# One instruction order for every engine at the start of a two-block model, and the last attention's mask as an identity matmul

## The chip, the core and the metric

The kernel runs on one core of a Trainium2 chip. The core has five engines with a queue of instructions each: TensorE (matmuls and their weight loads, PE and PEld in the profile), VectorE (DVE), ScalarE (ACT), GpSimd (POOL) and SyncE (SP, which issues DMAs). Each works through its queue in order and waits on semaphores for the others. The metric is the time of one execution in microseconds (us); lower is better.

## The reference

Two transformer blocks on 512 tokens with 1024 channels in float32. What matters here is the first line of the first block, a normalization of x, and the last mixer, a "stick-breaking" attention with 16 heads of 64 channels:

```python
def rms_norm(x, g):
    xf = x.astype(jnp.float32)
    xf = xf * lax.rsqrt(jnp.mean(xf * xf, axis=-1, keepdims=True) + EPS)
    return (xf * g.astype(jnp.float32)).astype(x.dtype)
# first block: h = rms_norm(x, norm1_g); z = h @ w_in; GLU and causal convolution, a dilated
# window attention (softmax), gates, then a feed-forward part. Second block: an attention on
# the 128 best keys, then this one:
def stick_breaking_mixer(x, w_in, w_out):
    q, k, v, g = jnp.split(x @ w_in, 4, axis=-1)        # each to 16 heads of 64
    z = jnp.einsum('bqhd,bshd->bhqs', qb, k) * HEAD_DIM_2 ** -0.5
    before = pos[None, :] < pb[:, None]                  # strictly earlier keys
    log_one_minus = jnp.where(before, jax.nn.log_sigmoid(-z), 0.0)
    log_stick = lax.cumsum(log_one_minus, axis=3, reverse=True) - log_one_minus
    a = jnp.where(before, jnp.exp(jax.nn.log_sigmoid(z) + log_stick), 0.0)
    o = jnp.einsum('bhqs,bshd->bqhd', a, v)
    return (o * jax.nn.silu(g)) @ w_out
```

## The kernel before

Activations stand as 8 tiles of 128 channels by 512 tokens. For accuracy each float32 operand is held as two float32r tiles, a rounded high part (`Ah`, `whi`) and the rest (`Al`, `wlo`), and a product of 128 by 512 takes 8 chunks of three matmuls each (high by high, high by low, low by high; L316 to L318). Weights come in 233 blocks, most of 512 KB, in the order of use: `Weights.load_one` issues the DMA on SyncE (L86), `split_one` rounds the block on ScalarE (`whi`, L118) and subtracts on GpSimd (`wlo`, L122). Two raw blocks and four split ones have room, so a block's load waits until the block two earlier is split.

TensorE's order is written out by hand: a `Stream` holds chunks of products, and `pull(n)` emits n of them. The other engines are ordered by the framework's scheduler, except in the GLU stage, where VectorE, ScalarE and GpSimd are fixed by hand as well.

**The start.** Constants are made (L218 to L236: `ident`, the `ones` matrices, the mask `before`, which holds -1e30 at and above a diagonal). SyncE loads two weight blocks, small vectors (L454 to L465), g1 and x (four tiles of 128 tokens). For each tile ScalarE sums the squares (L439) and forms 1/sqrt by Ln and Exp (L191), VectorE scales the tile (L442), TensorE transposes it (L444). Then ScalarE and VectorE evict the eight transposed tiles times g1 as `Ah` and `Al` (L447, L448). The first product of the GLU follows, then `columns()`, which transposes the small vectors (L474 to L487), and then 15 more products with the convolution's taps beside them on VectorE and GpSimd. VectorE also builds a window table `lnc` for the first attention (L783 to L794); the first gate's Tanh takes the memory of its temporaries.

**The last loop.** Eight pairs of heads run in `pair_loop`, one head a slot. A slot takes, in this order and with chunks pulled between the steps: the scores of query tile 0, a turn of the head before, scores 1, a turn, scores 2, a turn, a weighing, scores 3, two more weighings. A score step is two matmuls into PSUM (L568, L569, high and low part of the keys, 128 to 512 columns). Then VectorE adds the mask to the 128 columns on the diagonal (L643), ScalarE takes two Sigmoids, VectorE a scan (L648) and a multiplication (L649). A turn transposes these weights on TensorE (L580) and splits them (`PTh` on ScalarE, `PTl` on VectorE, L582 and L583); a weighing multiplies them with the values (L501). Scores have two PSUM banks, which come free with the second Sigmoid.

How many chunks are pulled after each of a slot's ten steps is a table, `PULLS`: 12 a slot (`P12`) for most slots, then 12, 12, 8 and 6 in the last four. What can be pulled are the projections q, k and v of the pair two ahead, and gate products, which are placed in that stream by `GATES3`. Gates 0 to 2 are computed ahead of the loop, in halves with the normalization, gates 3 to 5 as whole products behind them, and gates 6 and 7 in the stream of the last pair.

Of the kernel before, what the change touches and what calls it, by code (L numbers as in the profile page):

```python
# [10 lines left out]
F32 = mybir.dt.float32  # L11
# [28 lines left out]
GATES3 = ((0, 0), (6, 6), (6, 6), (6, 6), (6, 6), (6, 6), (6, 6), (6, 8))  # L40
# [3 lines left out]
PULLS = ((P12, P8, P8, P6, P6), (P12, P12, P12, P12, P12), (P12, P12, P12, P8, P6))  # L44
# [103 lines left out]
def model_kernel(ctx: ExitStack, tc: tile.TileContext, x, norm1_g, w_in, gate_b, conv_w, conv_b, conv_norm_g,  # L148
# [37 lines left out]
    ordered = {"load": None, "since": []}  # L186
    no_sync = mybir.DependencyInfo(mybir.DependencyClass.NoSync, mybir.DependencyReason.DATA)

    def act(o, i, func, **kw):

        ins = nc.scalar.activation(o, i, func, **kw).ins  # L191
        if ordered["load"] is not None:
            tc.add_manual_dep(ins, ordered["load"].name, no_sync)
        ordered["since"].append(ins)

    def act_tables(name):
        ordered["load"], since = None, ordered["since"]
        ordered["since"] = []
# [21 lines left out]
    before = const.tile([128, 128], F32, name="before")  # L220
    with tc.tile_pool(name="first", bufs=1) as first:
        jp = first.tile([128, 128], I32, name="jp")
        nc.gpsimd.iota(jp, pattern=[[1, 128]], base=0, channel_multiplier=-1)
        nc.gpsimd.tensor_scalar(ident, jp, 0.0, None, op0=OP.is_equal)
        nc.vector.memset(eps6, EPS)
        nc.vector.memset(eps5, LN_EPS / (ALPHA * ALPHA))
        zero128 = first.tile([128, 128], F32, name="zero128")
        nc.vector.memset(zero128, 0.0)
        nc.vector.tensor_scalar(ones_d, zero128, 1.0 / D, None, op0=OP.add)
        nc.vector.tensor_scalar(ones_h, zero128, 2.0 / D, None, op0=OP.add)  # L230
        nc.vector.tensor_scalar(ones_b, zero128, 0.0, None, op0=OP.add)
        for r in range(2):
            a = slice(64 * r, 64 * r + 64)
            nc.vector.tensor_scalar(ones_b[a, a], zero128[a, a], 1.0 / 64, None, op0=OP.add)
        nc.gpsimd.iota(jp, pattern=[[1, 128]], base=-127, channel_multiplier=1)
        nc.vector.tensor_scalar(before, jp, 0.0, NEG, op0=OP.is_le, op1=OP.mult)  # L236

# [39 lines left out]
    add_gates(w_in_b, range(GATES3[1][0]))  # L277
# [140 lines left out]
    g1 = const.tile([128, ND], F32, name="g1")  # L418
    hT = []
# [33 lines left out]
    for j in range(2):  # L453
        nc.sync.dma_start(cr[j], conv_w[0][:, 512 * j:512 * j + 512])  # L454
# [1119 lines left out]
```

## Time and profile before

| | us |
|---|---|
| median of 3 runs | 1619.07 (1616.58 to 1619.87) |
| the profiled execution, its own time | 1622.69 |
| its span, from the first to the last instruction | 1620.9 |
| TensorE busy in the span | 1525.0 (94%) |
| VectorE | 1132.4 (70%) |
| ScalarE | 846.7 (52%) |
| GpSimd | 811.8 (50%) |
| granted TensorE clock, mean | 0.978 of full speed |

A busy time is the union of an engine's instructions. Matmuls overlap in the record: in a dense stream one starts before the bar of the one ahead of it ends, so a busy TensorE is not one at its peak, and the starts tell its pace. A wait is the idle time in front of an instruction, put down to what released it last.

### The profile page before, as it was taken

What the parts mean: (1) busy time and instruction counts of PE and PEld (TensorE: products, weight loads), DVE (VectorE), ACT (ScalarE), POOL (GpSimd) and SP (SyncE); (2) the same over time, 40 slices, a digit from 0 to 9 for tenths busy, and PEclk for the clock granted to TensorE, in tenths of its full rate; (3) what the DMA queues carried; (4) which work ended last, traced back from release to release, by engine and by line L of the source; (5) the groups of instructions that cost most, each with busy time, mean ns of one, the idle gap of its engine ahead of it and who ended that gap; (6) DMA issues with size and microseconds to landing.
All of it is one profiled execution on the core that took longest, in us unless ns stands there. A gap on an engine that the chain in (4) does not pass through costs nothing.

```text
span 1620.9 us, 21268 instructions
## 1 busy us (share of the span) xinstructions
PE 1525.0 (94%) x7806; PEld 1289.3 (80%) x7806; DVE 1132.4 (70%) x1896; ACT 846.7 (52%) x1528; POOL 811.8 (50%) x680
## 2 busy tenths in 40 slices
PE   3999889999999999999999999999999789999996
PEld 3888778887778888888888887888887678887875
DVE  5899777786246567726735669988887753888874
ACT  4445677787553344423423444366765435666652
POOL 2679963333644554454444474445542875325314
PEclk8999999999999999999999999999999799999998
DMA  3323221212133423333333242322220313212212
GB/s 110 105 78 99 84 79 54 65 54 62 44 115 101 132 81 90 91 117 92 91 107 98 80 126 65 86 71 70 61 66 14 98 58 92 66 53 66 65 39 93
DMA packets 234604, 130.36 MB, mean 80 GB/s; under 512 B 5206, under 2 KB 232774, under 8 KB 234500
## 3 DMA queue, kind: packets, MB, share of 16 engines
q1 hardware_dynamic: 234356, 128.75, 27.2%
q8 instruction: 61, 1.00, 0.2%
q14 instruction: 43, 0.35, 0.1%
q10 hardware_dynamic: 144, 0.26, 0.0%
HBM read 126.90 MB, written 2.10 MB: 80 GB/s over the span
## 4 chain that ended last, share of the span: by engine, by line
PE 46%; DVE 28%; ACT 10%; issue 7%; POOL 6%; DMA 3%; DVEq 0%; ACTq 0%; POOLq 0%
PE pj L316 8%; PE pj L318 7%; PE pj L317 7%; PE s L317 5%; PE s L316 5%; PE s L318 5%; DVE pt L819 5%; POOL wlo L122 3%; DVE rest L648 2%; DVE PTl L583 2%; PE o L501 2%; ACT whi L118 2%; POOL S L825 2%; ACT k L547 2%; DVE q L522 2%
## 5 line engine op out<-in xcount | busy, mean ns | idle before, releaser
L122 POOL TENSOR_TENSOR wlo<-wraw,whi 128x256 fp32r<-128x256 f32 (+2 forms) x548 | 659.0, 1228 | 700.4 <-ACT whi L118 655.1
L316 PE MATMUL pj<-Ah,whi 128*128 128x512 f32 (+2 forms) x880 | 356.4, 405 | 19.7 <-DVE v L706 10.0
L118 ACT CAST whi<-wraw 128x1024 fp32r<-128x1024 f32 (+3 forms) x255 | 243.9, 966 | 217.2 <-PE pj L317 73.4
L318 PE MATMUL pj<-Ah,wlo 128*128 128x512 f32 (+2 forms) x880 | 345.1, 392 | 1.8 <-POOL wlo L122 1.8
L317 PE MATMUL pj<-Al,whi 128*128 128x512 f32 (+2 forms) x880 | 344.9, 392 | 0.0
L316 PEld LDWEIGHTS pj<-Ah,whi 128*128 128x128 f32 x880 | 169.2, 192 | 46.1 <-issue 9.2
L318 PEld LDWEIGHTS pj<-Ah,wlo 128*128 128x128 f32 x880 | 167.6, 190 | 38.6 <-POOL wlo L122 3.4
L317 PEld LDWEIGHTS pj<-Al,whi 128*128 128x128 f32 x880 | 168.5, 191 | 24.2
L317 PE MATMUL s<-Al,whi 128*128 128x512 f32 (+1 forms) x368 | 141.5, 384 | 3.7 <-DVE Al L1287 3.7
L316 PE MATMUL s<-Ah,whi 128*128 128x512 f32 (+1 forms) x368 | 141.3, 384 | 3.9 <-ACT Ah L1286 3.9
L318 PE MATMUL s<-Ah,wlo 128*128 128x512 f32 (+1 forms) x368 | 140.9, 383 | 0.0
L819 DVE SCALAR_TENSOR_TENSOR pt<-S,cw,pt 128x496 f32<-128x496 f32 (+19 forms) x180 | 124.8, 736 | 5.4 <-ACT pt L812 2.8
L340 PE MATMUL pj<-whi,Ah 128*128 128x256 f32 x384 | 112.8, 294 | 1.1 <-DVE q L522 1.1
L342 PE MATMUL pj<-whi,Al 128*128 128x256 f32 x384 | 108.5, 282 | 0.0
L341 PE MATMUL pj<-wlo,Ah 128*128 128x256 f32 x384 | 108.3, 282 | 0.0
L583 DVE TENSOR_TENSOR PTl<-pt,PTh 128x512 fp32r<-128x512 f32 x144 | 85.9, 598 | 29.9 <-ACT PTh L582 29.1
L191 ACT ACTIVATE P<-P,nm 128x128 f32<-128x128 f32 (+3 forms) x128 | 72.0, 563 | 63.4 <-DVE nm L613 62.6
L732 DVE SCALAR_TENSOR_TENSOR u<-ur,fw,u 128x511 f32<-128x511 f32 x44 | 74.9, 1705 | 37.6 <-ACT u L731 37.6
L825 POOL TENSOR_TENSOR S<-S,o 128x511 f32<-128x511 f32 (+29 forms) x60 | 78.2, 1317 | 15.7 <-ACT o L824 14.6
L580 PE MATMUL pt<-ident,P 128*128 128x128 f32 x480 | 78.8, 276 | 7.7 <-DVE P L649 5.7
L317 PEld LDWEIGHTS s<-Al,whi 128*128 128x128 f32 x368 | 70.5, 192 | 17.6 <-DVE Al L1287 4.5
L316 PEld LDWEIGHTS s<-Ah,whi 128*128 128x128 f32 x368 | 70.3, 191 | 17.5 <-ACT Ah L1286 4.5
(330 smaller groups left out, 3237.1 us busy)
## 6 DMA issues: line engine op xcount, KB each, us to landing
wraw<-in_w_in_dram SPq DMA_DIRECT2D x56, 512.0 KB
wraw<-in_w_up_dram SPq DMA_DIRECT2D x44, 512.0 KB
wraw<-in_w_in_a_dram SPq DMA_DIRECT2D x36, 512.0 KB
wraw<-in_w_in_b_dram SPq DMA_DIRECT2D x32, 512.0 KB
wraw<-in_w_down_dram SPq DMA_DIRECT2D x16, 512.0 KB
wraw<-in_w_attn_out_dram SPq DMA_DIRECT2D x8, 512.0 KB
wraw<-in_w_conv_out_dram SPq DMA_DIRECT2D x8, 512.0 KB
wraw<-in_w_out_dram SPq DMA_DIRECT2D x8, 512.0 KB
```

The costliest lines, as they stand in the source:

```text
L118: nc.scalar.copy(h, s)
L122: nc.gpsimd.tensor_sub(l[:, k], s[:, k], h[:, k].bitcast(F32))
L316: nc.tensor.matmul(o, hv[:, k, :], ah, start=first, stop=False)
L317: nc.tensor.matmul(o, hv[:, k, :], al, start=False, stop=False)
L318: nc.tensor.matmul(o, lv[:, k, :], ah, start=False, stop=last)
L340: nc.tensor.matmul(o, ah, hv, start=k == 0, stop=False)
L341: nc.tensor.matmul(o, ah, lv, start=False, stop=False)
L342: nc.tensor.matmul(o, al, hv, start=False, stop=k == 7)
L580: nc.tensor.transpose(pt[:, at:at + 128], self.P[r][:, k0:k0 + 128], ident)
L583: nc.vector.tensor_sub(l[:, :at], pt[:, :at], f32(h)[:, :at])
L819: nc.vector.scalar_tensor_tensor(o, a, w, o, op0=OP.mult, op1=OP.add)
L825: nc.gpsimd.tensor_add(o, o, t)
```

## The change

It has three parts.

1. At the start all five engines get their order by hand. SyncE issues g1 and x first, then two weight blocks, then the small vectors (a function `vectors()`). The making of constants moves behind these lines in the code, and a float32r copy of `ident`, `ident_r`, is added. Of the four squares ScalarE keeps tiles 0 and 2, and VectorE takes 1 and 3. The first block's rounding is written ahead of the evictions (`W.split_one()`). A table load for ScalarE moves behind the evictions.
2. In the last attention the mask is float32r, and a matmul of `ident_r` by `before` adds it in PSUM between the two score matmuls; the addition on VectorE is gone.
3. Gates 3, 4 and 5 move from ahead of the loop into its stream, and 11 slots pull 14 chunks in place of 12 (one more behind the third turn, one more behind the last weighing).

```diff
-GATES3 = ((0, 0), (6, 6), (6, 6), (6, 6), (6, 6), (6, 6), (6, 6), (6, 8))
+GATES3 = ((3, 3), (3, 3), (3, 4), (4, 5), (5, 5), (5, 6), (6, 6), (6, 8))
...
+P14 = (1, 1, 1, 1, 1, 2, 1, 1, 1, 4)
+PULLS = ((P12, P8, P8, P6, P6), (P12, P12, P12, P12, P12), (P14, P12, P12, P8, P6))
...
+    before = const.tile([128, 128], F32R, name="before")
+    ident_r = const.tile([128, 128], F32R, name="ident_r")
...
-    with tc.tile_pool(name="rows", bufs=1) as rows:
+    with tc.tile_pool(name="rows", bufs=1) as rows, tc.manual_schedule(engines={
+            mybir.EngineType.PE, mybir.EngineType.SP, mybir.EngineType.DVE, mybir.EngineType.Activation,
+            mybir.EngineType.Pool}):
         act_tables(LN_EXP)
+        xt = [rows.tile([128, D], F32, name=f"xt{t}") for t in range(NT)]
         g1r = rows.tile([ND, 128], F32, name="g1r")
         nc.sync.dma_start(g1r, norm1_g[0].rearrange("(a b) -> a b", b=128))
-        xt = []
         for t in range(NT):
-            xq = rows.tile([128, D], F32, name=f"xt{t}")
-            nc.sync.dma_start(xq, x[128 * t:128 * t + 128, :])
-            xt.append(xq)
+            nc.sync.dma_start(xt[t], x[128 * t:128 * t + 128, :])
         W.load_one()
         W.load_one()
+        vectors()
...
         for t in range(NT):
-            nc.scalar.activation(sq, xt[t], AF.Square, accum_out=ms[:, t:t + 1])
+            if t % 2 == 0:
+                nc.scalar.activation(sq, xt[t], AF.Square, accum_out=ms[:, t:t + 1])
+                nc.vector.tensor_tensor_reduce(out=sq2, in0=xt[t + 1], in1=xt[t + 1], scale=1.0, scalar=0.0,
+                                               op0=OP.mult, op1=OP.add, accum_out=ms[:, t + 1:t + 2])
...
+        W.split_one()
         for c in range(ND):
             h, l = act_pair(keep, "A", ND)
...
             nc.tensor.matmul(sc, qs[r][:, q0], ks[r][:, keys], start=True, stop=False)
+            if self.backwards:
+                nc.tensor.matmul(sc[:, :128], ident_r, before, start=False, stop=False, skip_group_check=True)
             nc.tensor.matmul(sc, qs[r][:, q0], kl[r][:, keys], start=False, stop=True)
...
-            nc.vector.tensor_add(sc[:, :128], sc[:, :128], before)
```

What this does to the instructions' order is shown at three places. The first is SyncE's queue at the very start; `S` tiles hold the small vectors, `xt` are the tiles of x. Before:

```order
L86 DMA wraw<-in_w_in_dram 128x8x128 x2
L454 DMA S_213<-in_conv_w_dram 31x512
L454 DMA S_214<-in_conv_w_dram 31x512
L458 DMA S_211<-in_gate_b_dram 16x128
L458 DMA S_211<-in_conv_b_dram 8x128
L458 DMA S_211<-in_conv_norm_g_dram 8x128
L458 DMA S_211<-in_norm_g_dram 8x128
L458 DMA S_211<-in_ln_g_dram 8x128
L458 DMA S_211<-in_ln_b_dram 8x128
L462 DMA S_211<-in_q_norm_g_dram 1x64
L423 DMA g1r<-in_norm_g_dram 8x128
L427 DMA xt_104<-in_x_dram 128x1024
```

The same queue in the changed program:

```order
L429 DMA g1r<-in_norm_g_dram 8x128
L431 DMA xt_91<-in_x_dram 128x1024
L431 DMA xt_92<-in_x_dram 128x1024
L431 DMA xt_93<-in_x_dram 128x1024
L431 DMA xt_94<-in_x_dram 128x1024
L87 DMA wraw<-in_w_in_dram 128x8x128 x2
L409 DMA S_83<-in_conv_w_dram 31x512
L409 DMA S_84<-in_conv_w_dram 31x512
L413 DMA S_81<-in_gate_b_dram 16x128
```

x moved from behind ten small vectors and two weight blocks to the second place; the third weight block stands behind all the vectors in both.

The second place is ScalarE's queue from the last square that it takes on. Before:

```order
L439 ACTIVATE sq,ms<-xt_110 128x1024
L191 ACTIVATE rs<-ms,eps_70 128x1
L191 ACTIVATE rs<-rs 128x1
L200 ACT_TABLE_LOAD
L447 ACTIVATE Ah<-pj,g_97 128x512 x2
L447 ACTIVATE Ah<-s,g_97 128x512 x2
L447 ACTIVATE Ah<-pt,g_97 128x512 x3
L447 ACTIVATE Ah<-o,g_97 128x512
L118 CAST whi<-wraw 128x1024 x3
```

The same queue in the changed program, where the square is that of tile 2:

```order
L462 ACTIVATE sq,ms<-xt_93 128x1024
L192 ACTIVATE rs<-ms,eps_70 128x1
L192 ACTIVATE rs<-rs 128x1
L192 ACTIVATE rs<-ms,eps_70 128x1
L192 ACTIVATE rs<-rs 128x1
L119 CAST whi<-wraw 128x1024
L473 ACTIVATE Ah<-pj,g_80 128x512 x2
L473 ACTIVATE Ah<-s,g_80 128x512 x2
L473 ACTIVATE Ah<-pt,g_80 128x512 x3
L473 ACTIVATE Ah<-o,g_80 128x512
L201 ACT_TABLE_LOAD
L119 CAST whi<-wraw 128x1024 x2
```

The first block's rounding moved ahead of the eight evictions, the other roundings and the table load stand behind them.

The third place is TensorE's queue in the middle of a slot of the last loop, from the second score step's end over the third turn (`pt`) to the weighing (`o`); `s` are scores, `pj` a product's chunk. Before:

```order
L569 MATMUL s<-kl_11920,q_12266 128x384
L316 MATMUL pj<-Ah,whi 128x512
L317 MATMUL pj<-Al,whi 128x512
L318 MATMUL pj<-Ah,wlo 128x512
L580 MATMUL pt<-ident,P 128x128 x2
L316 MATMUL pj<-Ah,whi 128x512
L317 MATMUL pj<-Al,whi 128x512
L318 MATMUL pj<-Ah,wlo 128x512
L501 MATMUL o<-PTh,v 128x512
```

The same stretch in the changed program, up to the weighing, which is the next row:

```order
L581 MATMUL s<-before,ident_r 128x128
L582 MATMUL s<-kl_11811,q_12157 128x384
L301 MATMUL pj<-Ah,whi 128x512
L302 MATMUL pj<-Al,whi 128x512
L303 MATMUL pj<-Ah,wlo 128x512
L593 MATMUL pt<-ident,P 128x128 x2
L301 MATMUL pj<-Ah,whi 128x512
L302 MATMUL pj<-Al,whi 128x512
L303 MATMUL pj<-Ah,wlo 128x512
L301 MATMUL pj<-Ah,whi 128x512
L302 MATMUL pj<-Al,whi 128x512
L303 MATMUL pj<-Ah,wlo 128x512
```

The identity matmul stands between the two score matmuls, and two chunks follow the turn in place of one.

## Rows read from the trace of the kernel before

**Rows 1.** Busy time by stretch: from:to, length, PE, PEld, DVE, ACT, POOL (instructions), PEclk, DMA.
```profile
40.00:160.00 120.00, 119.41 (x527) 98.21 (x526) 111.70 (x169) 60.46 (x85) 95.71 (x61) 1.00 0.32 93
...
160.00:240.00 80.00, 67.12 (x356) 57.25 (x355) 59.19 (x84) 55.97 (x98) 67.13 (x49) 0.94 0.27 79
...
1318.60:1335.00 16.40, 16.40 (x75) 13.57 (x74) 2.57 (x4) 6.84 (x9) 13.47 (x18) 1.00 0.33 97
...
1372.30:1519.40 147.10, 137.14 (x827) 118.67 (x826) 121.91 (x220) 95.51 (x202) 57.70 (x67) 1.00 0.19 56
```

**Rows 2.** Timeline, SyncE's issues: start, time, engine, line, what, idle before and who ended it.
```profile
0.73 1.06 SPq L86 DMA_DIRECT2D wraw<-in_w_in_dram  x2
...
12.17 1.78 SPq L427 DMA_DIRECT2D xt<-in_x_dram  x4
...
19.29 0.29 SPq L465 DMA_DIRECT2D S<-in_ffn_conv_b_dram  x1
...
32.06 26.30 SPq L86 DMA_DIRECT2D wraw<-in_w_in_dram  x7
```

**Rows 3.** Timeline of the head, all engines: from the first square to the third product.
```profile
15.78 1.06 ACT L439 ACTIVATE sq<-xt 128x1024 f32<-128x1024 f32 x1 [13.77 <-DMA xt<-in_x_dram]
...
20.91 1.04 ACT L439 ACTIVATE sq<-xt 128x1024 f32<-128x1024 f32 x1
...
23.92 1.27 ACT L447 ACTIVATE Ah<-pj,g 128x512 fp32r<-128x512 f32 x2
...
28.50 2.04 ACT L118 CAST whi<-wraw 128x1024 fp32r<-128x1024 f32 x2
...
29.67 4.87 POOL L122 TENSOR_TENSOR wlo<-wraw,whi 128x1024 fp32r<-128x1024 f32 x2 [27.25 <-ACT whi L118]
...
32.09 0.79 PE L318 MATMUL pj<-Ah,wlo 128*128 128x512 f32 x1 [1.23 <-POOL wlo L122]
```

**Rows 4.** Timeline of the head: two setup operations, the vectors' transposes, the first Tanh.
```profile
30.20 2.12 DVE L784 TENSOR_SCALAR lnc<-dist 128x512 f32<-128x512 f32 x1
...
36.31 0.43 DVE L789 TENSOR_SCALAR t<-dist 128x512 f32<-128x512 f32 x1
...
39.41 0.68 PE L474 MATMUL pt<-ident,S 31*128 31x31 f32 x8
...
42.34 0.60 ACT L191 ACTIVATE tmp<-pj 128x512 f32<-128x512 f32 x1 [5.62 <-DVE lnc L794]
```

**Rows 5.** Waits of TensorE: us, times, longest; 1372.3 to 1519.4, then 1519.4 to 1568.
```profile
PE o L501 <- DVE PTl L583: 4.9, 6, 1.4
PE pt L580 <- DVE P L649: 3.8, 4, 1.1
PE s L568 <- ACT P L191: 1.0, 2, 0.5
...
PE pt L580 <- DVE P L649: 1.9, 2, 1.5
```

**Rows 6.** Instructions on the mask's tile in the last loop: durations in ns, starts, shapes.
```profile
L643 DVE TENSOR_TENSOR s<-s,before x64: 271/290/300, 1363.2 to 1564.6; 128x128 f32<-128x128 f32 x64
```

**Rows 7.** Timeline in the last loop, TensorE and its weight loads around a narrow score.
```profile
1424.81 0.40 PE L317 MATMUL pj<-Al,whi 128*128 128x512 f32 x1
...
1425.04 0.39 PE L318 MATMUL pj<-Ah,wlo 128*128 128x512 f32 x1
...
1425.27 0.22 PE L568 MATMUL s<-k,q 128*128 128x128 f32 x1
...
1425.28 0.19 PEld L569 LDWEIGHTS s<-kl,q 128*128 128x128 f32 x1
...
1425.33 0.28 PE L569 MATMUL s<-kl,q 128*128 128x128 f32 x1
...
1425.38 0.19 PEld L316 LDWEIGHTS pj<-Ah,whi 128*128 128x128 f32 x1
...
1425.44 0.45 PE L316 MATMUL pj<-Ah,whi 128*128 128x512 f32 x1
```

More of the change, by code (lines that the diff above doesn't have):

```diff
@@ L184, in later @@
         tc.cur_priority = at
-    ordered = {"load": None, "since": []}
+    ordered = {"load": None, "since": [], "before": []}
     no_sync = mybir.DependencyInfo(mybir.DependencyClass.NoSync, mybir.DependencyReason.DATA)
@@ L191, in act @@
         ins = nc.scalar.activation(o, i, func, **kw).ins
-        if ordered["load"] is not None:
+        if ordered["load"] is not None and hT:
             tc.add_manual_dep(ins, ordered["load"].name, no_sync)
@@ L196, in act_tables @@
     def act_tables(name):
-        ordered["load"], since = None, ordered["since"]
-        ordered["since"] = []
+        ordered["load"], since = None, ordered["since"] or ordered["before"]
+        ordered["since"], ordered["before"] = [], since
         if name is not None:
@@ L276, in model_kernel @@
         W.add(w_out_a, 0, 8, 128 * c)
[L277 removed]
+    add_gates(w_in_b, range(GATES3[0][0]))
     for c in range(ND):
@@ L418, in model_kernel, with vectors @@
     g1 = const.tile([128, ND], F32, name="g1")
+    vr, fr, cr = kept()[:NV, :128], kept()[:88, :256].rearrange("p (a b) -> p a b", a=2), [kept()[:CW, :] for _ in range(2)]
+    def vectors():
+        for j in range(2):
+            nc.sync.dma_start(cr[j], conv_w[0][:, 512 * j:512 * j + 512])
+        r0 = 0
+        for src, n in ((gate_b[0], 16), (conv_b[0], 8), (conv_norm_g[0], 8), (norm2_g[0], 8),
+                       (ln_g[0], 8), (ln_b[0], 8)):
+            nc.sync.dma_start(vr[r0:r0 + n, :], src.rearrange("(a b) -> a b", b=128))
+            r0 += n
+        for i, src in enumerate((q_norm_g, k_norm_g)):
+            for j in range(2):
+                nc.sync.dma_start(vr[r0 + i:r0 + 1 + i, 64 * j:64 * j + 64], src)
+        for j in range(3):
+            nc.sync.dma_start(fr[44 * (j % 2):44 * (j % 2) + 44, j // 2, :], ffn_conv_w[0][j].rearrange("(a b) -> a b", b=128))
+        nc.sync.dma_start(fr[44:88, 1, :], ffn_conv_b[0].rearrange("(a b) -> a b", b=128))
@@ new lines, in model_kernel @@
+        nc.vector.memset(eps6, EPS)
+        nc.vector.memset(eps5, LN_EPS / (ALPHA * ALPHA))
+        zero128 = rows.tile([128, 128], F32, name="zero128")
+        nc.vector.memset(zero128, 0.0)
+        nc.vector.tensor_scalar(ones_d, zero128, 1.0 / D, None, op0=OP.add)
+        nc.vector.tensor_scalar(ones_h, zero128, 2.0 / D, None, op0=OP.add)
+        nc.vector.tensor_scalar(ones_b, zero128, 0.0, None, op0=OP.add)
+        for r in range(2):
+            a = slice(64 * r, 64 * r + 64)
+            nc.vector.tensor_scalar(ones_b[a, a], zero128[a, a], 1.0 / 64, None, op0=OP.add)
@@ L431, in model_kernel @@
+        nc.gpsimd.iota(jp, pattern=[[1, 128]], base=-127, channel_multiplier=1)
+        nc.vector.tensor_scalar(before, jp, 0.0, NEG, op0=OP.is_le, op1=OP.mult)
+        nc.vector.tensor_copy(ident_r, ident)
+        ms = rows.tile([128, NT], F32, name="ms")
+        rs = rows.tile([128, NT], F32, name="rs")
+        sq = rows.tile([128, D], F32, name="sq")
+        sq2 = rows.tile([128, D], F32, name="sq2")
         p = ps_o()
```

42 lines of the change are left out of this document (5 added, 37 removed).

## The prediction, made before the changed kernel was run

> **What bounds the kernel now.** I read the busy time by stage first, then who waits for whom, then the timeline of the two places that the diff touches. In the long middle TensorE is busy 119.41 of 120 us, and in the three gate products ahead of the last loop 16.40 of 16.40; in the last loop it is 137.14 of 147.10 with VectorE at 121.91 [rows 1]. So the middle gives back what the start gains, as long as no other engine's queue is late there, and the last loop is bound by TensorE with holes that VectorE makes. The start is bound by something else. The first tile of x is issued only 12.17 us in, after two weight blocks and ten small vectors [rows 2]; ScalarE squares from 15.78, the fourth square begins at 20.91, the transposed x is evicted from 23.92, both first weight blocks are rounded after that at 28.50, GpSimd makes their low parts from 29.67, and the third matmul, the first that needs a low part, starts at 32.09 [rows 3]. TensorE runs without a hole only from there.
>
> The middle is not touched. From the second GLU product to the end of the second attention, TensorE, GpSimd and SyncE have the same instructions in the same order in both programs, ScalarE and VectorE too once their setup is over. Two terms remain, the start and the last loop.
>
> **The change part by part: the start.** SyncE's first issues took 1.06 us for two, from 0.73 [rows 2]. Now g1 goes first and x second, so x is issued at about 1.05 in place of 12.17, 11.1 us earlier. The first square began 3.6 us after the issue (15.78 less 12.17), hence at 4.7 now; the fourth, at 20.91 [rows 3], becomes 9.8 if it keeps its distance to the issue (8.7 us). Halving ScalarE's squares gains little as long as the tiles arrive at that pace (three steps of 1.7 us); VectorE takes two of them, and I price them like ScalarE's, 1.1 us by its rows.
>
> From the fourth square to the first eviction took 3.0 us (20.91 to 23.92). Behind the last tile now stand VectorE's square, two exponentials and two scalings in a row: I add 0.8 for the second scaling. One weight block is rounded ahead of the evictions, 1.02 us (half of 2.04) [rows 3], partly while the last transposes run. So the first evicted pair is there at about 15.5, and the low part of that block, half of 4.87 or 2.4 us after its rounding, at about 15.5 as well. The third matmul starts near 16 in place of 32.09: 16.1 earlier. The other seven evictions follow at 0.64 us each (two in 1.27) [rows 3], and a chunk of three matmuls takes 0.69 at best (0.23 each) [rows 7]: they stay ahead.
>
> What this takes away must be covered elsewhere. The small vectors are now behind x and the weights. Their users, the transposes of `columns()`, stand behind the first product (24 matmuls) on TensorE: 39.41 before, about 23.3 now [rows 4]. The vectors' last issue came 7.1 us after the first x issue of before (19.29 less 12.17) [rows 2]; now two weight blocks and two conv pieces are in front of them as well, which I put at 20, landing at 22. That is just in time: 0 to 2 us. The third weight block is behind them on SyncE, so it is issued at 20 to 21 in place of 32.06 [rows 2], 12 earlier and not 16. With 3.6 to land, as x had, and 1.0 and 2.4 for its two parts it is ready near 27.5, and the third product wants it near 29.7 (24.2 behind the transposes, and 24 matmuls of 0.23): two us to spare.
>
> The Tanh of the first gate waited 5.62 us for VectorE's window tables (L794) at 42.34 [rows 4], and it still does, since it takes their memory; the next two roundings are queued behind it on ScalarE. These tables now have less time. Two operations on the same shape took 2.12 and 0.43 us, the long one while GpSimd ran a low part (29.67 to 34.5) [rows 3, 4]. If three of them are held up this way, they end 5 us later than if none is. The fourth product would then wait about 3 us for its weights, and the first convolution taps would start 13 rather than 16 us earlier. On this the Trainium skill has a rule, SBUF — State Buffer, section "Who interferes with whom": VectorE and GpSimd share a pair of ports as an exclusive lock, and the later of the two blocks until the other instruction ends. The two rows agree; by it the hold-up is a matter of which comes first, and the sum would be 3 us smaller.
>
> I take 16.1 less 0.6 for these thin places: **15.5 us**. Upwards 17 (x lands sooner with nothing in its way); downwards 11 (only the issue of x moves, and the rest is eaten by vectors, third block and tables).
>
> **The last loop.** Three gate products leave the stretch ahead of the loop, 16.40 us of unbroken TensorE work [rows 1], and are pulled inside it, 14 chunks a head in place of 12 for eleven heads. As work they cost the same there. They pay only as far as they fill holes. TensorE's holes: in the eleven heads that get the new count 4.9 + 3.8 + 1.0 = 9.7 us in twelve waits; in the last heads, whose counts stay, the largest group has 1.9 in two [rows 5]. A wait also breaks the overlap, since matmuls start every 0.23 us while their bars are 0.4 long [rows 7]: with up to 0.25 for each wait the holes are worth 12.7 and 2.4 us.
>
> The longest of them took 1.4 us, the mean is 0.8. Each now has one more chunk in front of it (three matmuls, 0.69 us), and VectorE is freed of 64 additions of 0.29 us [rows 6], 18.6 us of its own time, two of them between a turn and its weighing. That covers nearly all in the eleven heads: 12.7 becomes 1. In the last heads only the additions go: 2.4 becomes 1.4. What is late next there is VectorE's scan and multiplication, which no edit touches. The gates add 3 Tanhs and 3 products on VectorE to the loop, about 0.2 us a head, much less than is freed. Removed: 12.7.
>
> Against this stand 64 more matmuls on the engine that bounds the loop, and no row shows this one. The nearest: a score product of 128 columns starts at 1425.27, its partner at 1425.33, the next one at 1425.44 [rows 7]. So a 128-column product costs 0.06 us when its weights are already in, and 0.11 when they are not: the loads, at 1425.28 and 1425.38, come 0.11 apart. The 16 narrow scores have no cover for the additional load, 0.11; the other 48 have a longer matmul in front, 0.06: 1.8 + 2.9 = **4.7 us**, between 3.7 (64 x 0.058) and 7.0 (64 x 0.11). The Trainium skill gives a rule that speaks against the change, TensorE: Matmul & The Clock Gate, section "LDWEIGHTS (loading the stationary operand)": a load takes its columns at 1.2 GHz, 107 ns for 128, however long the matmul behind it. The spacing of the loads agrees (0.11), and if every identity matmul paid it, that would be 6.8 us.
>
> The loop gains 12.7 less 4.7, **8.0 us**; it lies between 0 (holes half filled, masks at 7.0) and 11 (all 15.1 of them filled, masks at 3.7). What precedes the loop keeps its pace: the first products now take the places of the gates in the weight queue.
>
> **The sum.** The profiled execution has 1622.69 us, of which the span is 1620.9. Less 15.5 and 8.0 it is 1599.2. It was 3.6 us above the median of the runs, 1619.07; against the median the sum is 1595.6, and I forecast 1596.
>
> **The rivals.** *The start gives only 11*, by the vectors, the third block or the held-up tables: 1619 - 11 - 8 = 1600. For it speaks how thin the margins become, against it that each of them needs several us of delay.
>
> *The loop gives nothing:* TensorE is its bound, the holes move behind the longer heads, and the masks are paid in full at 7.0. With half of the holes gone it is 15.1/2 - 7.0, about 0.5 us of gain: 1619 - 15.5 - 0.5 = 1603. The waits on VectorE speak for it, since a queue in fixed order can be late at another place; the 18.6 us that it loses speak against.
>
> *Slower:* the gain of the start is given back at 160 to 240, where TensorE is busy 67.12 of 80 us [rows 1] because VectorE and GpSimd are behind with the convolution. If their tables and taps end no sooner than before, being held up by each other, the whole 15.5 is lost there; with masks at 7.0 and no hole filled that is 1626. It decides only if VectorE's first tap does not move at all. Against it: before, the taps waited for the second product, which comes earlier.
>
> *The change doesn't do what it says:* SyncE's order is as written, but the loads of x wait for something else, and the start stays. 1619 - 8 = 1611.
>
> **How the numbers follow.** Forecast 0.66; start gives 11, 0.12; loop gives nothing, 0.14; slower 0.04; start stays, 0.04. The range of the likeliest runs from 17 + 11 = 28 off, 1591, to 11 + 3 = 14 off, 1605; the runs themselves spread over 3 us, and the second rival with a late start ends at 1607.5: 1589 to 1608. A run can tell about 0.2%, or 3.2 us, from no change. Slower by more than that is its rival alone, 0.04; within it a part of the last case and of chance, 0.03; faster the rest, 0.93.
>
> **What would show it.** Right: the first square near 5 us, the third matmul near 16, `columns()` near 23 without a wait, VectorE's first tap 14 to 16 us earlier. TensorE's idle time between 160 and 240, 12.9 us [rows 1], moves with it and stays. In the loop the heads of 14 chunks take 13.3 to 13.6 us with waits below 2 us in all, and no ScalarE wait for a mask. Wrong: a DMA or SyncE wait ahead of `columns()`; waits of the fourth product for its low part; waits for P or PTl in the loop of more than 6 us; an identity matmul that holds TensorE for more than 0.11.

## The result, and the profile after

The changed kernel takes 1600.38 us in the median (1598.51 to 1602.0, four runs) beside 1619.47 for the kernel before. The ratio is 0.9881 with a 95% interval of 0.9859 to 0.9903: 19 us faster, where 23.5 were forecast. Its profiled execution has 1601.03 us, of which the span is 1598.9.

Both programs have the same matmuls in the same order in the middle, so the start of each in one trace can be taken from its start in the other. TensorE is 16.25 us ahead of the kernel before at its third matmul, 18.4 at the end of the first product, 15.6 from 43 to 117, 13.67 at 300, and 12.70 at the last normalization ahead of the last loop (times of the kernel before). The 2.2 us that the first product adds are the clock: in the kernel before, the granted clock was 0.50 from 32 to 36, behind 5 us with hardly a matmul, and a matmul started every 0.43 us; in the changed kernel it is 1.00 there and one starts every 0.23. The loop and the tail give another 9.3 (321.3 us from there to the end before, 312.0 now). The sum is 22.0, the difference of the two spans (1620.9 and 1598.9). By the medians the gain is 3 us less. The profiled execution of before stands 3.2 us above its median and that of the changed kernel 0.65 above its own, so differences against the trace of before come out large. One run of the kernel with two masks took 2147.2 us at a granted clock of 0.655; it is left out below, and no other trace of that kernel exists.

Timeline of the changed kernel's start (start and length in us, engine, line, what, in brackets the idle time before and who ended it). The rows answer to [rows 3] and [rows 4].

```profile
5.06 1.06 ACT L462 ACTIVATE sq<-xt 128x1024 f32<-128x1024 f32 x1 [3.05 <-DMA xt<-in_x_dram]
...
15.84 0.39 PE L303 MATMUL pj<-Ah,wlo 128*128 128x512 f32 x1
...
19.80 1.06 ACT L119 CAST whi<-wraw 128x1024 fp32r<-128x1024 f32 x1
...
20.95 0.68 PE L485 MATMUL pt<-ident,S 31*128 31x31 f32 x8
...
22.00 1.86 DVE L799 TENSOR_SCALAR t<-ti 128x512 f32<-128x512 int32 x1
...
23.62 0.80 PE L303 MATMUL s<-Ah,wlo 128*128 128x512 f32 x1 [1.00 <-POOL wlo L123]
...
24.00 2.81 POOL L123 TENSOR_TENSOR wlo<-wraw,whi 128x1024 fp32r<-128x1024 f32 x1 [0.43 <-ACT whi L119]
...
24.50 2.33 DVE L490 TENSOR_SCALAR gate_half<-vec 128x16 f32<-128x16 f32 x1
...
30.91 0.60 ACT L192 ACTIVATE tmp<-pj 128x512 f32<-128x512 f32 x1 [6.99 <-DVE lnc L806]
...
33.29 0.78 ACT L824 ACTIVATE pt<-S,vec,cw 128x512 f32<-128x512 f32 x1
34.11 10.94 DVE L831 SCALAR_TENSOR_TENSOR pt<-S,cw,pt 128x511 f32<-128x511 f32 x14 [1.88 <-ACT pt L824]
```

The first square and the third matmul are within 0.4 us of where the prediction put them, and `columns()` comes 2.4 us earlier (20.95, without a wait). Then two things lose what was won. ScalarE rounds the second weight block at 19.80, behind eight evictions and a table load; TensorE waits for its low part at 23.62. And the window tables on VectorE end only at 30.8: a multiplication of 128x16 takes 2.33 us (0.18 before, at 42.73) while GpSimd makes a low part. The first gate's Tanh waits 6.99 us for them, two roundings stand behind it, and the activation that starts the convolution (L824) comes at 33.29. Before it started at 46.95:

```profile
46.95 0.78 ACT L812 ACTIVATE pt<-S,vec,cw 128x512 f32<-128x512 f32 x1 [2.13 <-DVE S L871]
```

It is 13.66 earlier, and TensorE is 13.67 ahead at 300.

TensorE's clock in three stretches of that start: from:to, length, busy time and count, granted clock, DMA share, GB/s. Behind the wait it is at its lower level, 1.2 GHz, in the whole of the second stretch; ahead of it and in the third it is at the higher one, 2.4 GHz.

```profile
16.00:22.00 6.00, 6.00 (x35) 1.00 0.31 89
24.20:26.80 2.60, 2.60 (x8) 0.50 0.68 198
28.00:34.00 6.00, 6.00 (x28) 1.00 0.30 88
```

At 104 TensorE meets the price. It wants a low part that GpSimd, in step with the convolution, makes 13.7 us earlier than before, and TensorE is 15.6 ahead (rows of the changed kernel's timeline, then GpSimd's low part before; there, TensorE's wait was 0.27):

```profile
101.44 2.37 POOL L123 TENSOR_TENSOR wlo<-wraw,whi 128x1024 fp32r<-128x1024 f32 x1
...
103.86 0.50 PE L303 MATMUL pj<-Ah,wlo 128*128 128x512 f32 x1 [2.15 <-POOL wlo L123]
```

```profile
115.09 2.41 POOL L122 TENSOR_TENSOR wlo<-wraw,whi 128x1024 fp32r<-128x1024 f32 x1
```

Busy time of each engine in the middle's weak stretch and in the eleven heads with the new count (columns as in [rows 1]). The idle time between 144 and 224 moved and stayed, 12.7 us; in these heads TensorE is busy 153.06 of 153.80 us. A full head takes 13.8 to 14.5 us.

```profile
144.00:224.00 80.00, 67.28 (x345) 57.17 (x344) 58.76 (x84) 56.63 (x99) 67.88 (x49) 0.94 0.28 81
1344.10:1497.90 153.80, 153.06 (x938) 135.94 (x937) 114.44 (x181) 99.88 (x206) 62.44 (x77) 1.00 0.22 62
```

What is left of TensorE's waits in those heads (us, times, longest), where [rows 5] had 9.7 us in twelve:

```profile
PE pt L593 <- DVE P L661: 0.7, 2, 0.4
```

An identity matmul in TensorE's timeline of the changed kernel. The three score matmuls start at 1403.89, 1404.07 and 1404.13, the next chunk at 1404.35:

```profile
1403.89 0.34 PE L579 MATMUL s<-k,q 128*128 128x384 f32 x1
1404.07 0.22 PE L581 MATMUL s<-before,ident_r 128*128 128x128 f32 x1
1404.13 0.39 PE L582 MATMUL s<-kl,q 128*128 128x384 f32 x1
1404.35 0.40 PE L301 MATMUL pj<-Ah,whi 128*128 128x512 f32 x1
```

It takes 0.06 us, but the matmul behind it takes 0.22 to the next start, where the same shape took 0.176 before (mean of ten). Over all 64: 59 ns for the identity and 52 more for the matmul behind it, or 111 and nothing with the narrowest scores. **The price is 0.111 us in either case, 7.1 in all**, the upper bound of the forecast and not its 4.7.

### The profile page after: what moved, and what is told of

Its sections match the earlier page's. It is cut to its first block, busy times and chain, and to the rows that moved or that the text cites. A ratio compares the mean times of both kernels' runs of the same rounds, so it can differ in the third digit from the quotient of the medians.

```text
span 1598.9 us, 21378 instructions
## 1 busy us (share of the span) xinstructions
PE 1527.2 (96%) x7870; PEld 1296.7 (81%) x7870; DVE 1121.4 (70%) x1837; ACT 845.4 (53%) x1524; POOL 806.5 (50%) x680
## 4 chain that ended last, share of the span: by engine, by line
PE 57%; DVE 23%; ACT 7%; POOL 5%; issue 5%; DMA 2%; DVEq 0%; SPq 0%; ACTq 0%; POOLq 0%
PE pj L301 10%; PE pj L302 9%; PE pj L303 9%; PE s L302 5%; PE s L303 5%; PE s L301 5%; DVE pt L831 5%; PE o L512 2%; POOL wlo L123 2%; PE pt L593 2%; PE pj L325 2%; PE pj L327 2%; PE pj L326 2%; POOL S L837 2%; DVE score L1442 1%
## 5 line engine op out<-in xcount | busy, mean ns | idle before, releaser
L301 PE MATMUL pj<-Ah,whi 128*128 128x512 f32 (+3 forms) x896 | 362.2, 404 | 15.2 <-DVE v L718 9.8
L303 PE MATMUL pj<-Ah,wlo 128*128 128x512 f32 (+3 forms) x896 | 350.4, 391 | 2.5 <-POOL wlo L123 2.5
L302 PE MATMUL pj<-Al,whi 128*128 128x512 f32 (+3 forms) x896 | 350.7, 391 | 0.0
L301 PEld LDWEIGHTS pj<-Ah,whi 128*128 128x128 f32 (+1 forms) x896 | 171.2, 191 | 41.9 <-issue 9.1
L303 PEld LDWEIGHTS pj<-Ah,wlo 128*128 128x128 f32 (+1 forms) x896 | 170.3, 190 | 39.1 <-POOL wlo L123 3.4
L302 PEld LDWEIGHTS pj<-Al,whi 128*128 128x128 f32 (+1 forms) x896 | 171.1, 191 | 24.4
L301 PE MATMUL s<-Ah,whi 128*128 128x512 f32 (+1 forms) x352 | 135.8, 386 | 4.0 <-ACT Ah L1298 4.0
L302 PE MATMUL s<-Al,whi 128*128 128x512 f32 (+1 forms) x352 | 135.7, 386 | 3.6 <-DVE Al L1299 3.6
L303 PE MATMUL s<-Ah,wlo 128*128 128x512 f32 (+1 forms) x352 | 135.6, 385 | 1.0 <-POOL wlo L123 1.0
L595 ACT CAST PTh<-pt 128x512 fp32r<-128x512 f32 x144 | 73.1, 513 | 19.6 <-PE pt L593 19.1
```

The source lines that it names most:

```text
L301: nc.tensor.matmul(o, hv[:, k, :], ah, start=first, stop=False)
L302: nc.tensor.matmul(o, hv[:, k, :], al, start=False, stop=False)
L303: nc.tensor.matmul(o, lv[:, k, :], ah, start=False, stop=last)
```

## The experiments

Each kernel is the changed one but for the edit shown, unless it says otherwise. "Convolution" is the start of the activation that opens it (L824 and its like), "at 300" how far TensorE is ahead of the kernel before when that is at 300 us, "loop and tail" the time from the last matmul on `ones_d` ahead of the last loop to the end of the span, all by the traces, in us. The ratio is to before as measured beside that kernel, where its median was 1617.9 to 1620.3.

| kernel | convolution | at 300 | loop and tail | median | ratio to before (95%) |
|---|---|---|---|---|---|
| before | 46.95 | 0 | 321.3 | 1619.5 | 1 |
| the changed kernel | 33.29 | 13.67 | 312.0 | 1600.4 | 0.9881 (0.9859 to 0.9903) |
| start alone | 33.67 | 12.46 | 321.5 | 1608.5 | 0.9932 (0.9906 to 0.9958) |
| additions on VectorE | 33.58 | 13.33 | 312.4 | 1598.3 | 0.9875 (0.9854 to 0.9896) |
| mask alone | 33.57 | 13.44 | 309.7 | 1597.6 | 0.9872 (0.9854 to 0.989) |
| two masks, mask alone | 33.24 | 13.88 | 317.0 | 1604.8 | 0.9907 (0.989 to 0.9925) |
| two masks | - | - | - | 1604.2 | 0.991 (0.9888 to 0.9931) |
| half the masks | 33.40 | 13.60 | 311.1 | 1599.0 | 0.987 (0.9856 to 0.9885) |
| two roundings | 33.98 | 12.84 | 312.3 | 1600.8 | 0.9886 (0.9869 to 0.9902) |
| tables and roundings | 31.11 | 16.01 | 312.5 | 1598.2 | 0.9864 (0.9849 to 0.9878) |
| squares on ScalarE | 33.82 | 12.26 | 312.2 | 1600.4 | 0.9877 (0.9848 to 0.9906) |
| vectors first | 42.55 | 4.49 | 312.3 | 1609.2 | 0.9933 (0.9911 to 0.9954) |
| mask alone, tables early | 31.20 | 15.09 | 309.8 | 1597.2 | 0.9859 (0.9839 to 0.9878) |
| half the masks, tables early, no filler | 31.06 | 15.73 | 312.7 | 1598.1 | 0.9863 (0.9843 to 0.9883) |

The medians have an uncertainty of 2 to 5 us, as much as most edits move; what is said of single edits below rests on the traces. Five of them have the changed kernel's last loop (its own, and those with two roundings, with tables and roundings, with the squares on ScalarE and with the vectors first): loop and tail take 312.0 to 312.5 us there, so differences of more than 0.5 count. Between 300 and the last loop the kernels drift by -1.0 to +2.6 us against the kernel before, with the same instructions there; what sets that was not tried.

### The loop: mask or filler

**The start alone.** The last loop of before under the new start.

```diff
-GATES3 = ((3, 3), (3, 3), (3, 4), (4, 5), (5, 5), (5, 6), (6, 6), (6, 8))
+GATES3 = ((0, 0), (6, 6), (6, 6), (6, 6), (6, 6), (6, 6), (6, 6), (6, 8))
...
-PULLS = ((P12, P8, P8, P6, P6), (P12, P12, P12, P12, P12), (P14, P12, P12, P8, P6))
+PULLS = ((P12, P8, P8, P6, P6), (P12, P12, P12, P12, P12), (P12, P12, P12, P8, P6))
...
-                nc.tensor.matmul(sc[:, :128], ident_r, before, ...)
...
+            nc.vector.tensor_add(sc[:, :128], sc[:, :128], before)
```

> The changed start with the last loop of before: the mask added on VectorE, gates 3 to 5 ahead of the loop, 12 chunks a head. Theory (the two parts add up, nothing that the start wins or loses depends on the loop): in the two profiles the instructions of TensorE run 12.7 us earlier than before at the end of the second attention, so 1619.5 - 12.7 = 1606.8, with the loop's waits for P and PTl as before (4.9 + 3.8 us). Rival (the start is worth the whole 15.5 us of the forecast and something in the changed loop takes 3 back): 1604. Rival (the parts need each other): 1600 to 1602.

The parts add up, as far as the drift lets it be told. Loop and tail take 321.5 us as before (321.3), with the waits of before, and the two traces are 13.9 us apart; with the 9.5 that the changed loop and tail gain against this kernel's, that is 23.4 against 22.0. The median says less: 1617.9 for before beside it, 1608.5 here, 9.4 us with an interval of some 4 to either side.

**The additions back on VectorE, with the filler.**

```diff
-                nc.tensor.matmul(sc[:, :128], ident_r, before, ...)
...
+            nc.vector.tensor_add(sc[:, :128], sc[:, :128], before)
```

> The changed kernel with VectorE's 64 additions of the mask in place of the 64 identity matmuls; gates 3 to 5 and the 14 chunks stay in the loop. Theory A (an identity matmul costs TensorE 0.111 us, the spacing of two weight loads, 0.059 before the next matmul and 0.052 behind it, and the filler alone closes the waits): 64 x 0.111 = 7.1 us faster than the changed kernel, 1593.3, with waits for P and PTl below 2 us. Theory B (the additions made the waits): each of the waits grows back by one or two additions of 0.29 us; with 11 to 24 waits that is 3 to 14 us against 7.1, 1596 to 1607.

Theory B. TensorE's waits there, from 1330 to the end of the loop:

```profile
PE pt L589 <- DVE P L658: 3.1, 4, 1.2
PE s L577 <- ACT P L192: 2.7, 3, 1.6
PE o L510 <- DVE PTl L592: 1.4, 3, 0.5
```

7.2 us of waits are back, about what the 64 matmuls cost, and loop and tail are the same (312.4 and 312.0). One more chunk ahead of each wait did not close them all. It did close a part: against the start alone, which has neither the filler nor the mask by matmul (321.5), the filler makes loop and tail 9.1 us shorter.

**The mask alone, without the filler.**

```diff
-GATES3 = ((3, 3), (3, 3), (3, 4), (4, 5), (5, 5), (5, 6), (6, 6), (6, 8))
+GATES3 = ((0, 0), (6, 6), (6, 6), (6, 6), (6, 6), (6, 6), (6, 6), (6, 8))
...
-PULLS = ((P12, P8, P8, P6, P6), (P12, P12, P12, P12, P12), (P14, P12, P12, P8, P6))
+PULLS = ((P12, P8, P8, P6, P6), (P12, P12, P12, P12, P12), (P12, P12, P12, P8, P6))
```

> The changed kernel with the mask by matmul, but without the filler: gates 3 to 5 ahead of the loop and 12 chunks a head, as before. Theory A (the filler closes the waits): of some 20 waits (18 us in the loop of before) each loses one or two additions of 0.29 us, 6 to 9 us, and the 64 matmuls cost 7.1: about the same as the start alone, 1604 to 1608, with 8 us of waits for P and PTl left. Theory B (the additions made the waits, the filler is not needed): the waits go to below 2 us and the time is that of the changed kernel, 1599 to 1601.

Theory B again, with a time even below its 1599 to 1601: in the whole loop TensorE waits for nothing (its view of waits from 1345 to the end of the loop is empty), every full head takes 12.4 to 12.6 us, and loop and tail are 2.3 us shorter than with the filler. So either edit alone gives what the two give together, or more, and once the additions are gone the filler costs time:

| loop and tail, us | 12 chunks, gates ahead of the loop | 14 chunks, gates in the loop |
|---|---|---|
| mask added on VectorE | 321.5 (start alone) | 312.4 |
| mask by matmul | 309.7 | 312.0 (the changed kernel) |

Why an addition of 0.29 us could make waits of 0.8 and more is seen at ScalarE. Its longest wait in the last loop, first before, then with the mask alone:

```profile
ACT rest L191 <- DVE s L643: 63.7, 39, 3.0
```

```profile
ACT rest L192 <- PE s L582: 24.0, 16, 2.8
```

The addition stood in VectorE's queue behind scans, multiplications and `PTl`. From the end of the second score matmul to the first Sigmoid 2.8 to 3.3 us passed before (means of 16 scores of each width), with the mask alone 0.4 to 1.3. Of the 2.8 to 3.3 us, 2.1 to 2.5 (means again) are from the end of the second score matmul to the start of the addition. So the addition's place in the queue delayed P, for which TensorE waited, by much more than 0.29. The edit also frees VectorE of 18.6 us of work; no run separates the two.

**Two masks.** The mask is added twice, first on the changed kernel, then on the one without the filler, where TensorE waits for nothing.

```diff
+                nc.tensor.matmul(sc[:, :128], ident_r, before, ...)
                 nc.tensor.matmul(sc[:, :128], ident_r, before, ...)
```

> The changed kernel with every identity matmul issued twice (the mask is added twice, which gives the same weights). Theory A (a narrow matmul costs the spacing of its weight load, 0.111 us): 64 x 0.111 = 7.1 us slower, 1607.5. Theory B (the step of the forecast: 0.06 us where a longer matmul stands ahead of it, 4.7 in all): 1605. Theory C (it costs nothing, since TensorE's stream has slack there): 1600.4.

> The kernel with the mask by matmul alone (no filler, 1597.6), with every identity matmul issued twice (the mask is added twice, which gives the same weights). There TensorE waits for nothing in the loop, so the price shows undisturbed. Theory A (a narrow matmul costs the spacing of its weight load, 0.111 us, 0.052 of it behind the next matmul): 64 x 0.111 = 7.1 us longer in the loop, 262.6 becomes 269.7, and 1604.7. Theory B (the step of the forecast, 0.06 with cover and 0.11 without): 4.7 us, 267.3 and 1602.3. Theory C (the second of a pair costs its columns alone, 0.059): 3.8 us.

The first gave 1604.2 us in the median of three runs, nearest to B (1605), but its interval of 3.5 us to either side takes in A (1607.5) too. The second decides for A: loop and tail take 316.95 in place of 309.68, 7.3 us or 0.114 for each, and the median moves from 1597.6 to 1604.8. TensorE's timeline of the second shows the pair: 0.06 from the first to the second, 0.11 from there to the score matmul, and 0.29 from that one to the next chunk, where 512 columns alone take 0.23:

```profile
1403.80 0.22 PE L581 MATMUL s<-before,ident_r 128*128 128x128 f32 x1
1403.86 0.27 PE L582 MATMUL s<-before,ident_r 128*128 128x128 f32 x1
1403.97 0.45 PE L583 MATMUL s<-kl,q 128*128 128x512 f32 x1
1404.26 0.40 PE L301 MATMUL pj<-Ah,whi 128*128 128x512 f32 x1
```

The Trainium skill, TensorE: Matmul & The Clock Gate, section "LDWEIGHTS (loading the stationary operand)", puts the nanoseconds of a load at its columns divided by 1.2: an estimate of 107 ns for 128 columns, and of 6.8 us for 64 loads. The trace agrees: the loads of this stretch start at 1403.80, 1403.91 and 1404.02, and the masks cost 7.1 to 7.3 us.

**Half the masks by matmul**, for query tiles 0 and 3, the other two on VectorE.

```diff
-            if self.backwards:
+            if self.backwards and qt in (0, 3):
...
+            if qt not in (0, 3):
+                nc.vector.tensor_add(sc[:, :128], sc[:, :128], f32(before))
```

> The changed kernel, with the identity matmul for query tiles 0 and 3 alone; tiles 1 and 2 get the mask on VectorE as before. Theory A (what makes the waits is the place of the addition in VectorE's queue, some 2.3 us from scores to Sigmoid in place of 0.29, and the filler has slack for half of them): 32 x 0.111 = 3.5 us faster than the changed kernel, 1596.9, with waits for P and PTl below 1 us. Theory B (each addition left brings its part of the waits back): half of the 9 us of waits that the addition on VectorE has with the filler return, 4.5 against 3.5 saved, 1600 to 1602.

In between: 32 matmuls fewer, 2.6 us of waits, loop and tail 0.9 us shorter than in the changed kernel.

### The start: what sets the taps

**The vectors first.** SyncE's order of before, everything else as changed: `rows_of_x` issues g1 and x, and `vectors` calls it behind its first `q_norm_g`.

```diff
-        nc.sync.dma_start(g1r, norm1_g[0].rearrange("(a b) -> a b", b=128))
-        for t in range(NT):
-            nc.sync.dma_start(xt[t], x[128 * t:128 * t + 128, :])
+
+        def rows_of_x():
+            nc.sync.dma_start(g1r, norm1_g[0].rearrange("(a b) -> a b", b=128))
+            for t in range(NT):
+                nc.sync.dma_start(xt[t], x[128 * t:128 * t + 128, :])
+
         W.load_one()
         W.load_one()
-        vectors()
+        vectors(rows_of_x)
...
+                if i == j == 0:
+                    then()
```

> The changed kernel with SyncE's issues in the order of before (two weight blocks, ten small vectors, then g1 and x). Theory A (the issue of x is the main part of the start's gain): first square at 15.8 and third matmul at 26.5, 10.7 later than in the changed kernel and 5.6 earlier than before; columns() near 31.6; the tables are done while VectorE waits for x, so the first taps start with the second product, near 40 to 42, against 34.1 and 47.8: 5 to 8 us slower than the changed kernel, 1605 to 1608. Theory B (it is the order of ScalarE, VectorE and GpSimd that counts): third matmul before 22, and within 3 us of the changed kernel.

Theory A, and somewhat more than it said: 8.8 us by the medians. Rows of its timeline:

```profile
15.20 1.06 ACT L467 ACTIVATE sq<-xt 128x1024 f32<-128x1024 f32 x1 [13.19 <-DMA xt<-in_x_dram]
...
25.21 0.40 PE L303 MATMUL pj<-Ah,wlo 128*128 128x512 f32 x1
...
40.17 0.60 ACT L192 ACTIVATE tmp<-pj 128x512 f32<-128x512 f32 x1 [9.03 <-DVE lnc L811]
...
42.55 0.78 ACT L829 ACTIVATE pt<-S,vec,cw 128x512 f32<-128x512 f32 x1
```

The tables were not made while VectorE waited for x, as I had expected; they stand behind the evictions in its queue. So everything is 9.3 us late, from the third matmul (25.21 and 15.84) to the taps (42.55 and 33.29). Of the 13.7 us of the start, SyncE's order has 9.2, and 4.5 are left for the order of the other engines.

**All squares on ScalarE.**

```diff
-            if t % 2 == 0:
-                nc.scalar.activation(sq, xt[t], AF.Square, ...)
-                nc.vector.tensor_tensor_reduce(out=sq2, in0=xt[t + 1], in1=xt[t + 1], ...)
+            nc.scalar.activation(sq, xt[t], AF.Square, ...)
```

> The changed kernel with all four squares on ScalarE. Theory (x arrives at 1.25 us a tile, a square with its two exponentials takes 1.6 on ScalarE, so the fourth scaling starts at 11.5 in place of 10.7): the third matmul at 16.6 in place of 15.84, and nothing of it at the end, since the window tables and not the second product set the first taps: 1600 to 1601. Rival (the third matmul's 0.8 us comes through): 1601.2.

The third matmul starts at 16.38 in place of 15.84, the median is the same (1600.4, two runs). The convolution starts 0.5 us later, and TensorE's lead at 300 is 12.3, just under the 12.5 to 13.9 that it has in the five other kernels whose start is that of the changed one: what the shared squares bring, if anything, is too small to be seen at the end.

**Two roundings ahead of the evictions.**

```diff
         W.split_one()
+        W.split_one()
```

> The changed kernel with the second weight block rounded ahead of the evictions as well, where ScalarE has 2.16 us of idle time. Both theories: the second product no longer waits for its low part at 23.62 (now 1.2 us, and 1.5 more at half the clock behind it). Theory A (VectorE's window tables are slow because GpSimd makes that low part beside them, with single operations of 0.4 us taking 1.9 to 2.5): the tables end at about 27 in place of 30.8, the first taps start 3 us earlier, and so does all that follows: 1597.4. Theory B (the tables take as long anyway): the taps stay at 34.1, the low part that is wanted at 104 waits the longer, and the time stays at 1600.4.

Neither. The second product no longer waits, but the first does, 4.19 us for `Al`. GpSimd and VectorE in the timeline of this run:

```profile
11.59 4.85 POOL L123 TENSOR_TENSOR wlo<-wraw,whi 128x1024 fp32r<-128x1024 f32 x2 [9.17 <-ACT whi L119]
...
11.72 2.52 DVE L799 TENSOR_SCALAR ti<-dist_i 128x512 int32<-128x512 int32 x1
14.16 2.56 DVE L796 CAST dist<-dist_i 128x512 f32<-128x512 int32 x1
16.64 1.40 DVE L475 SCALAR_TENSOR_TENSOR Al<-pj,g,Ah 128x512 fp32r<-128x512 f32 x2
```

TensorE in the same timeline:

```profile
17.43 0.51 PE L301 MATMUL pj<-Ah,whi 128*128 128x512 f32 x1 [4.19 <-DVE Al L475]
```

Two table operations of 0.43 and 0.41 us are held for one low part each, and the evictions stand behind them. With one rounding there had been one such operation there and time to spare. The Trainium skill, SBUF — State Buffer, section "Who interferes with whom", says that whichever of VectorE and GpSimd comes first holds the pair of ports that they share for its whole instruction, and the other blocks. The trace agrees: 2.52 and 2.56 against GpSimd's 2.4. The tables end at 31.5, 0.7 later than in the changed kernel, and the taps with them (33.98).

**The tables early as well.** Eight of the table's sixteen operations, GpSimd's iota among them, move ahead of the squares, the other eight behind the evictions; `dist` and `lnc` are allocated earlier for that.

```diff
+        nc.vector.tensor_copy(dist, dist_i)
+        nc.vector.tensor_scalar(lnc, dist, 128.0, None, op0=OP.is_le)
...
         for t in range(NT):
...
+        W.split_one()
         for c in range(ND):
```

> As the run with two roundings, and eight of the sixteen operations on the window tables moved to where VectorE waits for x (3.25 to 6.34 us). Theory A (Tanh of the first gate, and with it every tap, waits for the tables): tables end near 25, after which the second product decides: taps near 30 in place of 34.1, 4 us faster than the changed kernel, 1596.4. Theory B (it is the second product and not the tables that sets the taps): no better than two roundings alone. Theory C (the tables hold up VectorE's first square): the third matmul starts later than 15.84 and the gain is smaller than with two roundings alone.

Theory A in kind, but 2.3 us in size and not 4. Rows of its timeline, on ScalarE, GpSimd and VectorE:

```profile
11.59 4.70 POOL L123 TENSOR_TENSOR wlo<-wraw,whi 128x1024 fp32r<-128x1024 f32 x2 [9.05 <-ACT whi L119]
...
14.41 1.41 DVE L491 SCALAR_TENSOR_TENSOR Al<-pj,g,Ah 128x512 fp32r<-128x512 f32 x2 [3.05 <-ACT Ah L490]
...
27.72 0.60 ACT L192 ACTIVATE tmp<-pj 128x512 f32<-128x512 f32 x1 [3.74 <-PE s L303]
...
30.16 1.05 ACT L119 CAST whi<-wraw 128x1024 fp32r<-128x1024 f32 x1 [0.90 <-DMA wraw<-in_w_in_dram]
31.11 0.77 ACT L828 ACTIVATE pt<-S,vec,cw 128x512 f32<-128x512 f32 x1
```

The tables end at 27.5, Tanh comes 3.2 us earlier, but the activation that opens the convolution only 2.2: in ScalarE's fixed order it stands behind a rounding that waits for its block to land. TensorE is 2.3 us further ahead at 300 than in the changed kernel. The evictions, which read PSUM, take 0.70 each here beside a low part: those two do not hold each other up.

**Put together.** The mask without the filler, with the start of the run before (two roundings, tables early); then the same with half the masks.

> A kernel put together from what the runs showed: the mask by matmul without the filler (its last loop and tail took 309.7 us, with the filler 312.0), and the start with two blocks rounded ahead and half of the window tables early (it reached the last loop at 1283.4 in place of 1286.9). Theory (the two add up): 3.5 and 2.3 us, 1594.6 against the changed kernel's 1600.4. Rival (what the start gains is lost again by the middle, as the spread of the runs' starts of 2 us suggests): 1597 to 1598.

> As the run before it in this call, with the identity matmul for query tiles 0 and 3 alone. Theory A (32 x 0.111 = 3.5 us saved, and without the filler the waits of half of the additions return; half of the 15 us of waits that the start alone has would be 7 us): slower than with all masks by matmul, 1597 to 1599. Theory B (tile 3, whose weights are the last to be ready, makes nearly all the waits, so that the other additions are free): 1591 to 1592.

The first has the lowest time of all, 1597.2 us (0.9859), 3 us under the changed kernel. The sum of the two gains, 1594.6, did not come; the time is that of the rival (1597 to 1598). By the traces the loop's gain is there in full (309.8) and the convolution opens as early (31.20), but TensorE is 15.1 ahead at 300, where the same start had 16.0, and 14.6 at the last loop. And the intervals overlap, so that it beats the changed kernel is likely and not shown. The second is no better: without the filler the additions left bring 3.1 us of waits back, and loop and tail go from 309.8 to 312.7, theory A.

## Why the prediction was right, and where it was not

The time lies in the range, 4.4 us above the forecast. It equals that of a rival, *the start gives only 11* (1600), and part of the reason is that rival's too, the held-up tables.

**The start: right up to the evictions, mis-sized behind them.** Forecast and measured: first square 4.7 and 5.06, third matmul 16 and 15.84, `columns()` 23.3 and 20.95, taps "13 rather than 16 us earlier" if the tables are held up, and 13.66 (the sign asked for 14 to 16). The price of the hold-up was worked out, but the sum did not take it: 15.5 should have been about 13.5. The step that failed is "I take 16.1 less 0.6 for these thin places". In the changed program's order the tables share the time with two low parts, so that the hold-up was the likely case and not the outer one. Where it would be paid was wrong too: the fourth product did not wait 3 us for its weights; the lead stayed at 15.6 until 117 and fell at the low part that comes in step with the convolution. The runs with the tables early and with the vectors first show it from both sides: TensorE's lead at 300 follows the first tap within 0.9 us, over leads from 4.5 to 16, and not the third matmul (with two roundings that came 2.3 us later and the tap 0.7). The wait of the second product, 1.2 us and 1.6 more at half the clock, was not foreseen (only the third block was looked at); it costs nothing at the end, because the taps are later still. Nor were the 2.2 us that the first product gains by the clock; for the same reason they bring nothing at the end.

**The loop: right in size, with two terms too small.** Forecast 8.0, measured 9.3. The masks cost 7.1 and not 4.7: the term took cover by a longer matmul for granted, but what the cover hides of the identity's load is paid at the matmul behind. So 16.4 us of waits and broken overlap went, where 12.7 were put down. That the chunk and the freed VectorE together cover "nearly all in the eleven heads" came true, 0.7 us of waits are left. But the holes were more: of the last heads the forecast counted the largest group alone. TensorE's waits in the whole loop before:

```profile
PE pt L580 <- DVE P L649: 5.7, 6, 1.5
PE o L501 <- DVE PTl L583: 5.4, 7, 1.4
PE s L568 <- ACT P L191: 1.6, 3, 0.6
```

That is 12.7 us in sixteen waits, or 16.7 with the forecast's 0.25 for each, and nearly all of it went; the 1.4 of 2.4 that the forecast left to VectorE's scan in the last heads went too. What the forecast did not see is that the edits replace each other. The mask by matmul alone leaves no wait, the filler alone leaves 7.2 us, and the filler beside the mask makes the loop 2.3 us longer. That 8.0 lies near 9.3 is in part luck: the holes were 3.7 us too small and the masks 2.4 too cheap. A full head takes 13.8 to 14.5 us, over the sign's 13.3 to 13.6.

**The sum.** By the traces it is 22.0 against 23.5: the start, 12.7 at the last loop, was put 2.8 us too high and the loop 1.3 too low, and that these cancel in part is luck. The rest of the miss, some 3 us, lies between traces and medians: the terms were read from an execution 3.6 us above the median and taken off the median, while the changed kernel's profiled execution stood 0.65 above its own. In which stage these 3 us lie no run shows.

**The rivals.** *The loop gives nothing* had the masks' price right (7.0) and the holes wrong. *Slower* did not come, since VectorE's first tap moved. *The start stays* fell with the first square.

## What to carry to other kernels

Price a small operation on another engine by its queue: from what it waits for to what waits for it, not by its own duration. Here 0.29 us stood for more than 2 us of latency, and taking it off that engine closed every hole, where more filler closed a part. Try two cures for the same wait one at a time: here each was worth 9 to 12 us alone, and the second added nothing to the first. A narrow matmul between longer ones cost TensorE 0.11 us here, the spacing of two weight loads, half of it on the instruction behind. And when a start is made faster, look for the engine with the least idle time behind it, here the taps' chain through VectorE's tables and ScalarE's order: its first instruction told the gain, not TensorE's.

## What the runs showed of the hardware

- An identity matmul of 128 columns cost TensorE 0.111 to 0.114 us amid matmuls of 512 columns that start 0.227 apart (in the changed kernel, and two masks with the mask alone). Loads of narrow matmuls start 0.11 apart there, so that each long matmul has 0.117 to spare; that spare time did not take up the additional load.
- VectorE operations of 0.18 to 0.43 us on SBUF took 2.3 to 2.6 beside GpSimd's subtraction (2.4), two in a row in the run with two roundings; evictions from PSUM took 0.70 beside the same subtraction.
- After 1.0 us of waiting at 23.6 TensorE's granted clock was 0.50 from 24.2 to 26.8, and matmuls started every 0.43 us instead of 0.23.
